# Own buffers for twiddles and sums in the Fourier pairs, the tail ahead of the next prework in the forward scan, and fold loads a block ahead

## The chip, the cores and the metric

The kernel runs on one core of a Trainium2 chip. The metric is the device time of one execution in microseconds (us). Engines are named as the profile names them: PE is the matrix engine, PEld its weight loads, DVE the vector engine, ACT the scalar (activation) engine, POOL the third one, and SP issues nearly all DMA transfers, in order, from one queue.

## The reference

One layer of an encoder, with a sequence of L = 2048 tokens and width D = 1024, in float32:

```python
h = rmsnorm(x, norm_g) * (1 + scale) + shift          # shift, scale, gate from silu(c) @ w_ada
u_f, z_f, q, k, v, r, gf_low, gb_low = split(h @ w_in)
y_f = fourier_mix(u_f, w_fmap) * silu(z_f)
y_g = gla_mix(q, k, v, gf_low, gb_low, ...) * silu(r)
x = x + gate * (concat(y_f, y_g) @ w_out)
return rmsnorm(x, final_g)
```

`fourier_mix` takes, for each of 4 groups of 256 columns, the real part of a two-dimensional Fourier transform over tokens and columns and multiplies it by a 256 x 256 map. `gla_mix` is gated linear attention with 4 heads in chunks of 64 tokens, with one scan forward and one backward over the tokens; its gates are log-sigmoids of a low-rank projection, and its output is normalized by head.

## The kernel before

**Precision and matmuls.** Matmuls run on operands split into a high and a low part (`A_hi`, `A_lo`), three passes for a product (`PASSES`). The input projection is done in bulk blocks with a seven-product scheme: `block_col` (L273, 84 matmuls of 128x512 in a block, 12 for each of the seven products) and `block_tok` (L316). Results come out of PSUM tiles `pj` through ACT and DVE. Tokens are handled in two halves, m = 1 (tokens 1024 to 2047) first, then m = 0.

**Stages.** In the order of the code: gate vectors and normalized x; `do_v(1, A, 0)`, the first half of the value projection of half 1; two calls of `fold`, which multiply the column Fourier table by the group maps (32 matmuls each, L394) and store the result in `fold_d`; `gate_sums`; `do_v(1, A, 1)`; `gate_row`; then q, k, z, r of half 1 with the first four blocks of the backward scan (`scan_back`, blocks 7 to 4) between them; then u of both halves; then the Fourier stage; the value, query and key projections of half 0; the other four blocks of the backward scan (3 to 0) with the r projection between them (`do_r`), the splitting of the output weights and first output products (`out_fourier`); and last the forward scan with the output projection.

**Order.** A list scheduler puts the instructions of all engines into an order of its own, guided by the code's order and by data and buffer dependences; so bulk matmuls of a later projection stand among those of a Fourier pair where the pair has to wait. Each engine then runs its instructions strictly in that order. All loads and stores go through SP's queue in order as well.

**The Fourier stage.** For each group g, `stage1` does additions on DVE, `do_z` projects the group's gate, and `fourier(g, Z)` runs over five pairs of residues (`PAIRS`). A step of a pair loads two operands `us` (L42), multiplies them by twiddle factors (two ACT instructions at L699 and L700, two on DVE at L701 and L702), splits the result into `gp`, multiplies by the sequence table (`pq`) and splits that into `PQ`. A pair then multiplies by the folded map `wm` into `mapA`, copies half of it (`cm`, ACT at L741), adds and subtracts (L742, L743) and multiplies both into the gate tiles Z (L744, L745). The tiles `tw` (products of a twiddle), `cm`, `wmst` (a map being staged) and `tabstg` (the table being staged) share one tag "T" with two buffers. `us0` has two buffers, `us1` one.

**The scans.** `prework` (L483 to L541) makes the decayed q and k of a block of 256 tokens for one pair of heads: a gate matmul `lg` (L491), Abs, Exp and Ln on ACT into `pa`, a running sum on DVE, and three more Exps. `pin_exp_ln` loads the table set that has both Exp and Ln; it is called in the first prework of each half's backward scan (blocks 7 and 3), and after each Silu of `sr` in blocks 8 to 15 of the forward scan. The forward scan runs over 16 blocks of 128 tokens, sc = 0 to 15: `core_fwd` (scores `sc`, outputs `on` at L766 and L768, state updates `upd`), a prework for the next 256 tokens at odd sc, `out_fwd` for the block before (48 output matmuls `po` at L836, or 96 where the Fourier half wasn't added ahead; `ahead` holds 0, 2, 5, 8, 11 and 15), and `tail_fwd`: Square on ACT with a sum, `rstd` on POOL, scaling of `o` (L804), four transposes for each pair of heads (`otr`, L808), the product with the gate tile `sr` (L810), and the split into `ghi` and `glo`. `sr` has one buffer. Table loads appear on ACT as ACT_TABLE_LOAD; the compiler puts one wherever the function needed isn't in the set that is loaded.

## Time and profile before

| | us |
|---|---|
| median of three runs | 1791.66 (1790.52 to 1793.68) |
| the profiled execution | 1784.68 |
| its span | 1782.9 |
| PE busy | 1597.6 (90%) |
| DVE busy | 1180.1 (66%) |
| ACT busy | 633.0 (36%) |
| POOL busy | 62.4 (4%) |

The profiled execution is one run with the hardware profiler on; its span runs from the first to the last record. Busy time counts the instructions that do work. "PEclk" is the share of full clock that was granted to TensorE in a stretch: a matmul takes longer where it is below 1. In the rows that list waits, the time is idle time of the waiting engine ahead of an instruction, with what ended it behind the arrow.

### The profile page before, as it was taken

To read this page: it belongs to the slowest core of one execution; us is meant where nothing else is said; L and a number is where in the kernel's file an instruction comes from. 1 tells how busy PE (TensorE), PEld (TensorE's weight loads), DVE (VectorE), ACT (ScalarE), POOL (GpSimd) and SP (SyncE) were. 2 spreads that over 40 slices of the span, in tenths; PEclk is the share of its full clock that TensorE was granted. 3 is DMA by queue.
4 is the path that set the end of the run, shared out by engine and by line. 5 is a ranking of instruction groups with operands and counts; after the bars stand their busy time and mean duration, and the time that the engine had idled before them with its cause. 6 is when DMAs were issued, how large, how long until landed. Compare 5 with 4: busy or idle time off the path is not lost. (4 is left out here: it accounts for less than half of the span.)

```text
span 1782.9 us, 25115 instructions
## 1 busy us (share of the span) xinstructions
PE 1597.6 (90%) x9012; PEld 1370.6 (77%) x9012; DVE 1180.1 (66%) x2423; ACT 633.0 (36%) x1245; POOL 62.4 (4%) x118
## 2 busy tenths in 40 slices
PE   5879899999989999999889999379998979897996
PEld 2569678778889979889878887358877868776885
DVE  4963578887579266786845454797875765677473
ACT  3632244343245011213232232663433333454342
POOL 0000000000000000000000000000010101001010
PEclk9999999999999999999999999569999989998998
DMA  7496688878975898879796867766553433434321
GB/s 286 174 402 236 245 316 307 287 281 299 349 284 203 269 337 304 270 259 328 232 300 189 283 206 234 251 206 192 182 163 108 153 96 114 146 95 133 116 89 59
DMA packets 220188, 400.42 MB, mean 225 GB/s; under 512 B 19488, under 2 KB 121632, under 8 KB 216480
## 3 DMA queue, kind: packets, MB, share of 16 engines
q1 hardware_dynamic: 219920, 398.56, 66.0%
q8 instruction: 71, 1.16, 0.3%
q14 instruction: 53, 0.43, 0.1%
q10 hardware_dynamic: 144, 0.26, 0.0%
HBM read 238.13 MB, written 160.63 MB: 224 GB/s over the span
## 5 line engine op out<-in xcount | busy, mean ns | idle before, releaser
L273 PE MATMUL pj<-A_hi,B 128*128 128x512 f32 x1344 | 438.4, 402 | 13.9 <-ACT B L48 11.3
L316 PE MATMUL pj<-B,A_hi 128*128 128x264 f32 (+1 forms) x1792 | 333.2, 287 | 17.5 <-DVE B L49 5.0
L273 PEld LDWEIGHTS pj<-A_hi,B 128*128 128x128 f32 x1344 | 253.3, 190 | 74.7 <-ACT B L48 13.1
L316 PEld LDWEIGHTS pj<-B,A_hi 128*128 128x128 f32 x1792 | 281.4, 191 | 22.1 <-DVE B L49 6.0
L273 PE MATMUL pj<-A_lo,B 128*128 128x512 f32 x672 | 268.4, 399 | 0.0
L316 PE MATMUL pj<-B,A_lo 128*128 128x264 f32 (+1 forms) x896 | 254.6, 286 | 2.3 <-DVE A_lo L49 2.3
L316 PEld LDWEIGHTS pj<-B,A_lo 128*128 128x128 f32 x896 | 171.4, 192 | 2.5 <-DVE A_lo L49 2.5
L273 PEld LDWEIGHTS pj<-A_lo,B 128*128 128x128 f32 x672 | 127.7, 190 | 27.5
L836 PE MATMUL po<-wo_hi,fhi 128*128 128x512 f32 x256 | 104.9, 411 | 9.2 <-ACT po L865 6.8
L836 PE MATMUL po<-wo_hi,ghi 128*128 128x512 f32 x256 | 105.1, 411 | 0.0
L836 PE MATMUL po<-wo_lo,ghi 128*128 128x512 f32 x256 | 103.6, 405 | 0.0
L836 PE MATMUL po<-wo_lo,fhi 128*128 128x512 f32 x256 | 102.9, 402 | 0.0
L836 PE MATMUL po<-wo_hi,flo 128*128 128x512 f32 x256 | 100.4, 403 | 0.2 <-DVE flo L49 0.2
L573 DVE SCALAR_TENSOR_TENSOR state<-state,sm,upd 128x256 f32<-128x256 f32 x112 | 48.6, 475 | 60.1 <-PE upd L56 59.8
L836 PE MATMUL po<-wo_hi,glo 128*128 128x512 f32 x256 | 84.0, 403 | 0.4 <-DVE glo L49 0.4
L277 DVE TENSOR_TENSOR u<-u,pj 128x512 f32<-128x512 f32 x96 | 65.5, 683 | 27.0 <-PE pj L273 24.6
L581 ACT ACTIVATE vh<-v 128x512 fp32r<-128x512 f32 x64 | 40.2, 628 | 106.3 <-PE upd L56 97.6
L48 ACT ACTIVATE B<-raw 128x512 fp32r<-128x512 f32 x72 | 42.8, 624 | 88.4 <-DMA raw<-in_w_in 35.0
L321 DVE TENSOR_TENSOR u<-u,pj 128x264 f32<-128x264 f32 (+1 forms) x96 | 48.6, 513 | 37.6 <-PE pj L316 37.3
L551 PE MATMUL sc<-qi,ki 128*128 128x128 f32 x256 | 58.2, 312 | 13.3 <-DVE ki L520 5.1
L56 PE MATMUL mapA<-PQ,wm 128*128 128x256 f32 x480 | 65.0, 284 | 5.0 <-DVE PQ L49 3.6
L56 PEld LDWEIGHTS mapA<-PQ,wm 128*128 128x128 f32 x480 | 61.9, 190 | 8.5 <-DVE PQ L49 4.1
(216 smaller groups left out, 3009.9 us busy)
## 6 DMA issues: line engine op xcount, KB each, us to landing
bcol_d<-B SPq DMA_DIRECT2D x84, 512.0 KB, 4.2
B<-bcol_d SPq DMA_DIRECT2D x84, 512.0 KB, 4.8
v<-v_d SPq DMA_DIRECT2D x64, 256.0 KB, 3.1
btok_d<-B SPq DMA_DIRECT2D x28, 528.0 KB, 4.0
B<-btok_d SPq DMA_DIRECT2D x28, 528.0 KB, 5.9
btok_d<-B SPq DMA_DIRECT2D x28, 512.0 KB, 4.6
B<-btok_d SPq DMA_DIRECT2D x28, 512.0 KB, 6.0
raw<-in_w_in SPq DMA_DIRECT2D x12, 1024.0 KB, 7.7
```

The lines of the kernel that those rows point to most:

```text
L48: S.activation(hi, src, AF.Copy)
L56: T.matmul(ps, a, b, start=(k == 0), stop=(k == n - 1))
L273: T.matmul(ps[:], B[k][0][:, bq, p, :], A[k][aq][:, p, :], start=(p == 0 and q == 0), stop=(p == 3 and q == 2))
L277: V.tensor_tensor(o, a, ps[:], ALU.add)
L316: T.matmul(ps[:, j, :], A[k][aq][:, p, t * P:(t + 1) * P], B[k][p // 2][:, bq, p % 2, :], start=(p == 0 and q == 0), stop=(p == 3 and q == 2))
L321: V.tensor_tensor(o[:, cut], a[:, cut], ps, ALU.add)
L551: T.matmul(ps[:, h, 0:128], ki[:, c0:c0 + P], qi[:, c0:c0 + P], start=True, stop=True)
L573: V.scalar_tensor_tensor(state[:, h, :], state[:, h, :], dec[:, g:g + 1], up_[:, h, :], ALU.mult, ALU.add)
L581: S.activation(vh[:], v[:], AF.Copy)
L836: T.matmul(ps[n][:], a, wo[j0 + j][q][:, cs], start=(first and a is yh and q == 0), stop=(last and a is yl))
```

## The change

It has four parts.

The three vectors of the first stage become slices of one tile `vecs`; the twiddle table is loaded into it later and the tile `tw` of the Fourier stage goes. The table is transposed on the way in to fit.

In the Fourier pairs `cm` gets a tag of its own with two buffers and two slots (the difference is written over the copy), so that only `tw`, `wmst` and `tabstg` share "T"; `tabstg` shrinks to 512 columns and is loaded in two pieces; `us0` goes from two buffers to one.

The fold is cut into `fold_load`, with two buffers and both loads right behind the first half of the value projection, and `fold`, which stands behind the second half.

In the forward loop `tail_fwd` follows `core_fwd` at once; its split is a function of its own, `split_y`, called after the next block's core; `out_fwd` comes last.

```diff
-    gs = cp.tile([P, KT], F32, name="gs")
-    shift = cp.tile([P, KT], F32, name="shift")
-    cact = cp.tile([P, KT], F32, name="cact")
+    vecs = cp.tile([P, 3, KT], F32, name="vecs")
+    gs, shift, cact = (vecs[:, n] for n in range(3))
...
-    def fold(gg, gw):
-        fin = gw.tile([P, 2048], F32, tag="fold", name="fold_in")
+    def fold_load(gg, gw):
+        fin = gw.tile([P, 2048], F32, tag="fold", name="fold_in", bufs=2)
...
+        return tabs, wf
+
+    def fold(gg, tabs, wf):
...
     def fourier(g, Z):
-        thi, tlo, tw = fconst["thi"], fconst["tlo"], fconst["tw"]
+        thi, tlo = fconst["thi"], fconst["tlo"]
...
-                us = [fp.tile([P, 256], F32, tag=f"us{n}", name="us", bufs=2 - n) for n, sl in enumerate(SLOT[l1]) if sl is not None]
+                us = [fp.tile([P, 256], F32, tag=f"us{n}", name="us") for n, sl in enumerate(SLOT[l1]) if sl is not None]
...
-                    c_, s_, n_ = (tw[:, l1 - 1, q:q + 1] for q in range(3))
+                    c_, s_, n_ = (vecs[:, q, l1 - 1:l1] for q in range(3))
...
-                cm = fp.tile([P, 3, 2, P], F32, tag="T", name="cm", bufs=2)
+                cm = fp.tile([P, 2, 2, P], F32, tag="cm", name="cm", bufs=2)
                 S.activation(cm[:, 0, 0:np_, :], bv, AF.Copy)
                 V.tensor_tensor(cm[:, 1, 0:np_, :], av, cm[:, 0, 0:np_, :], ALU.add)
-                V.tensor_tensor(cm[:, 2, 0:np_, :], av, cm[:, 0, 0:np_, :], ALU.subtract)
+                V.tensor_tensor(cm[:, 0, 0:np_, :], av, cm[:, 0, 0:np_, :], ALU.subtract)
                 V.tensor_tensor(z1, z1, cm[:, 1, 0:np_, :], ALU.mult)
-                V.tensor_tensor(z2, z2, cm[:, 2, 0:np_, :], ALU.mult)
+                V.tensor_tensor(z2, z2, cm[:, 0, 0:np_, :], ALU.mult)
...
     def tail_fwd(sc, os_, sr):
-        halves = []
...
             V.tensor_tensor(y, tp[:], y, ALU.mult)
+        return sr
+
+    def split_y(sr):
+        halves = []
+        for hp in range(2):
+            y = sr[:, 4 * hp:4 * hp + 4, :]
             hi = op.tile([P, 4, P], F32R, tag="ghi", name="ghi", bufs=3)
             lo = op.tile([P, 4, P], F32R, tag="glo", name="glo", bufs=2)
             split(hi[:], lo[:], y)
...
     do_v(1, A, 0)
     gw = pool(glate, "gate")
-    for g in range(2):
-        fold(g, gw)
+    folds = [fold_load(g, gw) for g in range(2)]
     acc = gate_sums(gw)
     do_v(1, A, 1)
+    for g in range(2):
+        fold(g, *folds[g])
     gate_row(acc, gw)
...
-    tw = fp.tile([P, 8, 3], F32, name="tw")
-    tabstg = fp.tile([P, 640], F32, tag="T", name="tabstg", bufs=2)
-    load(tabstg[:], i["seqtab"])
-    load(tw[:], i["tw"])
-    split(thi[:], tlo[:], tabstg[:])
-    fconst.update(thi=thi, tlo=tlo, tw=tw)
+    for cs in (slice(0, 512), slice(512, 640)):
+        tabstg = fp.tile([P, 512], F32, tag="T", name="tabstg", bufs=2)[:, 0:cs.stop - cs.start]
+        load(tabstg, i["seqtab"][:, cs])
+        split(thi[:, cs], tlo[:, cs], tabstg)
+    load(vecs[:], i["tw"])
+    fconst.update(thi=thi, tlo=tlo)
...
-    pending = None
+    sr = None
     for sc in range(16):
         if sc:
             os_ = core_fwd(sc, pre, st_f)
+            ys = split_y(sr)
+        sr = tail_fwd(sc, os_, load_sr(sc))
         if sc % 2 and sc != 15:
             gt = gates(sc // 2 + 1)
             pre = [prework(0, sc // 2 + 1, hp, gt) for hp in range(2)]
-        if pending is not None:
-            out_fwd(*pending)
-        pending = (sc, tail_fwd(sc, os_, load_sr(sc)), None if sc in ahead else load_yf(sc))
-    out_fwd(*pending)
+        if sc:
+            out_fwd(sc - 1, ys, None if sc - 1 in ahead else load_yf(sc - 1))
+    out_fwd(15, split_y(sr), None)
```

What the scheduler makes of it stands in the compiled order of each engine. PE, where the bulk projections end and the second backward scan begins, before: `pj` are bulk products, `lg`, `sc`, `ob` and `upd` belong to the scan.

```order
L273 MATMUL pj<-A_hi,B 128x512 x2
L273 MATMUL pj<-A_lo,B 128x512
L273 MATMUL pj<-A_hi,B 128x512
L491 MATMUL lg<-gt,wab_10023 128x256 x4
L551 MATMUL sc<-qi,ki 128x128
L601 MATMUL ob<-state_10036,Q 128x256 x2
L552 MATMUL sc<-Q,K 128x64
```

After, in the middle of the same scan, five of whose eight units lie in this manner among bulk products:

```order
L272 MATMUL pj<-A_hi,B 128x512 x2
L272 MATMUL pj<-A_lo,B 128x512
L272 MATMUL pj<-A_hi,B 128x512 x2
L603 MATMUL ob<-state_10038,Q 128x256 x2
L272 MATMUL pj<-A_lo,B 128x512
L272 MATMUL pj<-A_hi,B 128x512 x2
L272 MATMUL pj<-A_lo,B 128x512
L272 MATMUL pj<-A_hi,B 128x512
L493 MATMUL lg<-gt,wab_10024 128x256 x2
L56 MATMUL upd<-vh,kth 128x256
L56 MATMUL upd<-vl,kth 128x256
```

The last product of a Fourier pair (`mapA`) had 70 bulk matmuls behind it and has 460 now, and the scan's first units moved in among those.

ACT in the first preworks of that scan, before (`wo_hi` are output weights being split, `vh` values):

```order
L494 ACTIVATE pa<-lg 128x512
L481 ACT_TABLE_LOAD
L581 ACTIVATE vh<-v 128x512
L497 ACTIVATE pa<-pa 128x512
L581 ACTIVATE vh<-v 128x512
L498 ACTIVATE pa<-pa 128x512
L511 ACTIVATE sm<-sm 128x8
L475 ACTIVATE gt<-gf 128x256
L513 ACTIVATE pa<-pb 128x512
L518 ACTIVATE pb<-pb 128x512
```

After, the same preworks, with Silu of the r projection's results (L356) between them:

```order
L496 ACTIVATE pa<-lg 128x512
L483 ACT_TABLE_LOAD
L499 ACTIVATE pa<-pa 128x512
L356 ACT_TABLE_LOAD
L356 ACTIVATE st<-st 128x512
L500 ACT_TABLE_LOAD
L500 ACTIVATE pa<-pa 128x512
L477 ACTIVATE gt<-gf 128x256
L356 ACT_TABLE_LOAD
L356 ACTIVATE p_10166<-p_10166 128x512
L513 ACT_TABLE_LOAD
L513 ACTIVATE sm<-sm 128x8
```

One table load stood there and now there is one at nearly every change between Silu, Exp and Ln; in the whole program there are 68 where there were 20, 26 of the new ones in this scan and 22 in the forward scan's first half.

PE at the end of the program, where block 14's output products (`ghi`, `glo`) meet block 15's transposes (`otr`), before:

```order
L836 MATMUL po<-wo_hi_11726,glo 128x512 x2
L836 MATMUL po<-wo_hi_11726,ghi 128x512
L836 MATMUL po<-wo_lo_11727,ghi 128x512
L836 MATMUL po<-wo_hi_11726,ghi 128x512
L836 MATMUL po<-wo_lo_11727,ghi 128x512
L836 MATMUL po<-wo_hi_11726,glo 128x512 x2
L808 MATMUL otr<-ident,o 128x128 x8
L836 MATMUL po<-wo_hi_11696,ghi 128x512
L836 MATMUL po<-wo_lo_11697,ghi 128x512
L836 MATMUL po<-wo_hi_11696,ghi 128x512
```

After, the first and the second group of transposes of block 15:

```order
L768 MATMUL on<-vh,sl 128x256
L770 MATMUL on<-state_11740,Q 128x256
L843 MATMUL po<-wo_hi_11697,glo 128x512
L809 MATMUL otr<-ident,o 128x128 x4
L843 MATMUL po<-wo_hi_11697,ghi 128x512
L843 MATMUL po<-wo_lo_11698,ghi 128x512
L843 MATMUL po<-wo_hi_11697,ghi 128x512
L843 MATMUL po<-wo_lo_11698,ghi 128x512
L843 MATMUL po<-wo_hi_11697,glo 128x512 x2
```

```order
L843 MATMUL po<-wo_lo_11718,ghi 128x512
L843 MATMUL po<-wo_hi_11717,ghi 128x512
L843 MATMUL po<-wo_lo_11718,ghi 128x512
L843 MATMUL po<-wo_hi_11717,glo 128x512 x2
L809 MATMUL otr<-ident,o 128x128 x4
L843 MATMUL po<-wo_hi_11727,ghi 128x512
L843 MATMUL po<-wo_lo_11728,ghi 128x512
L843 MATMUL po<-wo_hi_11727,ghi 128x512
```

The eight transposes stood together behind all products of block 14; now 30 of those products lie between the two groups of four, and 12 behind the second.

More of the change, by code (lines that the diff above doesn't have):

```diff
@@ L899, in hybrid_kernel @@
         load(gcol[:], i["gla_g"])
-        S.activation(cact[:], ccol[:], AF.Silu)
+        S.activation(cact, ccol[:], AF.Silu)
         KO(V.tensor_scalar(b1[:], bcol[:, :, 1], 1.0, None, ALU.add))
@@ L1119, in _tables @@
     f = lambda z: np.ascontiguousarray(z, dtype=np.float32)
-    return {"seqtab": f(seq), "tw": f(tw), "chtab": f(ch), "mask": np.concatenate([mask, mask], axis=1),
+    return {"seqtab": f(seq), "tw": f(tw.transpose(0, 2, 1)), "chtab": f(ch), "mask": np.concatenate([mask, mask], axis=1),
             "sel": f(sel), "ident": np.eye(P, dtype=np.float32)}
```

## The prediction

> **What bounds the kernel now.** I read the page's engine shares and slices first, then busy time by stretch of the program, then what TensorE waits for, and last the instructions around the longest waits.
>
> ```profile
> span 1782.9 us, 25115 instructions
> PE 1597.6 (90%) x9012; PEld 1370.6 (77%) x9012; DVE 1180.1 (66%) x2423; ACT 633.0 (36%) x1245; POOL 62.4 (4%) x118
> ...
> PE   5879899999989999999889999379998979897996
> ...
> PEclk9999999999999999999999999569999989998998
> ```
>
> TensorE is busy for 90% of the span; no other engine passes 66%. 185 us are left in which PE is idle, and the slices show where: the start, one place near three fifths of the way (digits 3 and 7, with a clock of 5 and 6), and a long tail of eights. The change adds and removes no matmul, so all it can win is PE idle time and time at a low clock. By stretch (columns: length; busy time of PE, PEld, DVE, ACT, POOL; granted clock; DMA share; GB/s):
>
> ```profile
> 113.90:144.00 30.10, 17.07 (x68) 14.20 (x67) 12.25 (x16) 10.98 (x20) 0.00 (x0) 0.77 1.03 390
> 144.00:186.00 42.00, 42.00 (x341) 41.17 (x339) 16.60 (x37) 9.52 (x18) 1.64 (x1) 1.00 0.45 172
> 694.00:937.00 243.00, 225.72 (x1571) 209.10 (x1571) 175.07 (x466) 60.15 (x115) 0.00 (x0) 0.99 0.85 275
> 937.00:1111.00 174.00, 173.91 (x917) 147.78 (x915) 86.18 (x167) 47.94 (x91) 0.00 (x0) 1.00 0.72 228
> 1111.00:1196.00 85.00, 41.38 (x175) 34.08 (x175) 73.38 (x136) 53.95 (x93) 0.00 (x0) 0.65 0.73 239
> ...
> 1340.00:1745.00 405.00, 365.54 (x1838) 304.73 (x1838) 264.44 (x550) 163.00 (x370) 48.48 (x91) 0.95 0.37 116
> 1745.00:1782.90 37.90, 22.48 (x92) 17.52 (x90) 11.77 (x19) 9.48 (x21) 4.04 (x10) 0.85 0.15 53
> ```
>
> The first two rows are the map fold and the rest of the value projection; the next two the Fourier stage and the bulk projections behind it; 1111 to 1196 is the start of the second backward scan; the last two are the forward scan and its end. The costliest row by far is 1111 to 1196: 43.6 us without a matmul, and the rest at a clock of 0.65, while DVE works 73 of the 85 us. The longest single waits of PE lie in the same stretches (columns: total, times, longest):
>
> ```profile
> PE pj L394 <- DMA fold_in<-in_w_fmap: 13.0, 1, 13.0
> ...
> PE lg L491 <- DMA v<-v_d: 17.3, 1, 17.3
> PE lg L491 <- DVE pa L499: 5.0, 1, 5.0
> ...
> PE otr L808 <- DVE o L804: 12.3, 2, 6.7
> PE on L766 <- ACT sh L48: 8.2, 2, 5.2
> PE otr L808 <- DVE sr L810: 5.9, 4, 2.2
> ```
>
> **Part A, the fold.** Both loads now go out together and the 64 fold matmuls stand behind the whole value projection.
>
> ```profile
> 113.86 7.07 PE L394 MATMUL pj<-fold_in 128*128 128x256 f32 x32
> 133.96 10.08 PE L394 MATMUL pj<-fold_in 128*128 128x256 f32 x32 [13.03 <-DMA fold_in<-in_w_fmap]
> ```
>
> The second fold waits 13.03 us for a load that could only be issued when the first fold had read the single buffer, and then runs 3.01 us longer than the first, at the clock that the pause left (0.77 over the stretch). Bound of the gain: 13.03 + 3.01 = 16.0 us. Against it: DMA is saturated here (share 1.03, 390 GB/s), so the bytes of the value projection's weights, which now have to be there some 20 us earlier, were themselves on the way. I give back 5 us, a third of the bound: the stretch's DMA time is fully used, but only the part of its bytes that comes after the fold's is needed earlier. The fold's eight stores now stand in SP's queue just ahead of the gate row's; in the 42 us after 144 the DMA share is 0.45, which hides them. Moving the fold to where the projection is over costs its 14 us of matmuls there instead of here: nothing. **A = -11 us, ends -16 and 0.**
>
> **Part B, the Fourier pairs and what follows them.** Own buffers change which instruction a pair waits for. In the pairs now, ACT waits for the mapped sums ahead of the next pair's twiddles:
>
> ```profile
> ACT cm L741 <- PE mapA L56: 88.1, 32, 6.6
> ...
> ACT tw L699 <- DVE Z L745: 11.5, 13, 2.2
> SPq L42 <- ACT tw L700: 25.5, 14, 5.0
> us<-us_d SPq DMA_DIRECT2D x61, 128.0 KB, 4.2
> 694.00:1096.00 402.00, 384.72 (x2424) 345.23 (x2424) 256.15 (x623) 105.44 (x201) 0.00 (x0) 1.00 0.79 254
> 1097.00:1110.00 13.00, 13.00 (x57) 10.49 (x56) 1.00 1.02 297
> ```
>
> 88.1 us of ACT's time go into 32 waits of that kind, and the twiddle that follows waits for the last use of the shared buffer (L745). PE loses little by it, because bulk projections fill the gaps (384.7 of 402 us busy, clock 1.00); but it spreads the pairs so far that the last map product comes 70 bulk matmuls ahead of the end of the bulk. In the new order 460 stand behind it. One costs 13.0 / 57 = 0.228 us, so the pairs must end 390 x 0.228 = 89 us of PE work earlier, and those bulk matmuls then lie beside five of the eight units of the backward scan, which had none. That fills the stretch 1111 to 1196. Its 41.38 us of matmuls at clock 0.65 are 27 us at full clock; with some work at the edges that can't be hidden I count 30. Bound of the gain: 85 - 30 = 55 us; other end 0, where everything won here is lost in the pairs.
>
> What eats of it. (1) The pairs are now packed into 384.7 - 89 = 296 us of PE work. DVE's share of the old stretch is 256 us; the 89 us of bulk that leave take 89 x 16.60 / 42.00 = 35 us of DVE with them, so 221 us of DVE stand beside 296 of PE, 75%. The nearest row is 694 to 937, where DVE has 72% and PE idles 17.3 of 243 us (7%). 7% of 296 is 21 us against the 17.3 that are lost now; with the higher density I take 10 us more than now. (2) One buffer for the first operand of a twiddle: the other operand has had only one all along, so the load of each step already waits for a read; a load costs 4.2 us to landing and up to 1.8 of waiting in the queue (25.5 / 14), 36 steps x 6.0 = 216 us, inside 296. I cost it at 0, with the DVE-bound cycle as its cover; without that cover it's a rival below. (3) Three units remain behind the bulk, and the scan units among it contain new table loads, next. I take 12 us for both, about a fifth of the stretch, the nearest row being the units that had no bulk at all. The staged table is loaded in two pieces, once, ahead of the first pair, with bulk on PE: 0. The in-place subtract and the twiddles' new home change no count: 0. **B = -55 + 10 + 12 = -33 us, ends -55 and 0.**
>
> **Table loads.** Because Silus of the gate projection and the scan's Exp and Ln now alternate on ACT, the compiled order has 68 table loads where it had 20: 26 more in the backward scan, 22 in the first half of the forward scan, two in the chain of each prework there.
>
> ```profile
> 1747.04 1.28 ACT L791 ACT_TABLE_LOAD   x1 [4.78 <-DMA sr<-r_d]
> 1748.33 1.06 ACT L791 ACTIVATE sr<-sr 128x1024 f32<-128x1024 f32 x1
> 1749.41 1.28 ACT L481 ACT_TABLE_LOAD   x1
> ```
>
> 48 x 1.28 = 61 us more on ACT, which rises from 633 to about 695 us. ACT is idle for two thirds of the span, so this costs only where a chain of ACT, DVE and PE is the limit. In the forward scan a prework is covered by the 96 output matmuls of a block (22 us at 0.23), and its two extra loads are 2.6 us: mostly hidden, 6 us taken in C.
>
> The Trainium skill, page "ScalarE: Activation LUTs", section "What ACT_TABLE_LOAD costs", states about 1283 ns for the load and about 1380 ns of drain, 2.66 us for a switch; by that the 48 would be an estimated 128 us of ACT. The trace agrees with the 1283 ns, but beside these loads it has no second gap: the next instruction starts 0.01 us after a load and the next load 0.02 us after an instruction. So the sum goes by 1.28.
>
> **Part C, the forward scan.** The tail (norm, transposes, gate) now follows the block's core at once, ahead of the next prework; the hi/lo split of its result comes after the next core; the output matmuls come last.
>
> ```profile
> 1752.64 0.61 PE L836 MATMUL po<-wo_hi,glo 128*128 128x512 f32 x2
> 1759.95 1.09 PE L808 MATMUL otr<-ident,o 128*128 128x128 f32 x4 [6.69 <-DVE o L804]
> 1761.82 1.11 PE L808 MATMUL otr<-ident,o 128*128 128x128 f32 x4 [0.79 <-DVE sr L810]
> ```
>
> At the end PE finishes block 14's products, waits 6.69 us for the last normalized rows, then 0.79 us, and starts the last 48 products at a reduced clock. Now 30 products of block 14 stand between the two groups of transposes of block 15 and 12 behind the second: (30 + 12) x 0.23 = 9.7 us of cover where there was none. What is late next is the gate's tile: `sr` has one buffer, its load waits until block 14's result is split, and that split now comes after block 15's core:
>
> ```profile
> sr<-r_d SPq DMA_DIRECT2D x16, 512.0 KB, 3.6
> L791 ACT ACT_TABLE_LOAD x8 | 10.3, 1283 | 27.4 <-DMA sr<-r_d 27.4
> ```
>
> From the split on, the load takes 3.6 us, and two table loads and the Silu 1.28 + 1.06 + 1.28 = 3.6; the second group's Square stands behind them on ACT, and normalizing and transposing it takes some 3 us more (an estimate: two DVE rows and POOL). That is 10 us against the first transposes' 1.1 and 30 products' 7 us, so about 2 us of waiting remain: -5.5, and -0.5 from the clock. Of the other waits of the tail (12.3 - 6.7 = 5.6 for o, 5.1 for sr) and the 8.2 for the split scores I take half, -9; the loop's 39.5 idle us (405 - 365.54) are of many kinds, so the low end for the whole of C is -25. Against it stand +6 for the table loads. For the later split I count +1: in every block the same 10 us chain has 96 output products (22 us) as its cover, or 48 (11 us) in the six blocks whose Fourier half was added ahead. Without that cover the chain's 10 us would fall on each block; upper end +15, one us a block. **C = -6 - 9 + 7 = -8 us, ends -25 and +15.**
>
> **Sum.** -11 - 33 - 8 = -52 us. The profiled execution took 1784.7 us (span 1782.9 and 1.8 around it), so 1733 for such a one. The median of the runs shown, 1791.7, is 7.0 us above it: 1740.
>
> **Rivals.** (R1) The pairs don't get denser on the chip. For it: DVE would be at 75% beside loads that hold the SP queue; the step's budget is 296 / 36 = 8.2 us, and load and wait take 6.0 of it, so at 8.2 us a step the loads set the pace, and what is won in the scan is idle PE in the pairs. Then B is 0 and the sum is A and C: 1784.7 - 19 = 1766, 1773 as a median. Against it: the old order was slowed by a chain through ACT, not by DVE.
> (R2) Slower: the table loads lie on the path. In the backward scan PE takes its instructions in order, with bulk behind each scan matmul; if a prework that waits for tables holds up the next scan matmul, the bulk waits as well. Without tables the sum would be about -52 - 18 = -70 us (6 in C and 12 in B taken back). 48 loads spend that at 1.46 us each, 1.28 and 0.18 of hand-over; at 1.7 us the time is 1784.7 + 48 x 1.7 - 70 = 1796, 1803 as a median. For it: two loads in every prework's chain. Against it: PE has bulk or output matmuls ahead of nearly every one of them; in the first backward scan, with bulk between the units and no tables, PE is 98% busy:
>
> ```profile
> 222.00:445.00 223.00, 218.38 (x1053) 179.53 (x1052) 180.92 (x347) 92.28 (x186) 0.00 (x0) 0.99 0.84 298
> ```
>
> By the Trainium skill's 2.66 us ("ScalarE: Activation LUTs", "What ACT_TABLE_LOAD costs"), with every switch on the path, the estimate would be 128 - 70 = 58 us slower; the trace's rows above speak for the smaller price.
> (R3) The forward scan takes back what A and B give, by the chain over the single `sr` buffer: 44 / 15 = 2.9 us more for each block decide it, and then the time is the old one. For it: ACT already waits 27.4 us for these loads in 8 blocks. Against it: the cover above.
>
> **How the numbers follow.** The forecast's own case (-75 to -32 against the time before) gets 0.64; a larger gain, B and C near their bounds, 0.08; R1 and what lies near it, from -32 to -4 us, 0.18; no change, R3, 0.04; R2 0.06. A measurement of this kernel can tell about 0.2%, 3.6 us. Faster 0.90, same 0.04, slower 0.06. The range for 8 in 10 leaves out R2, R3 and the extreme gains: 1706 to 1778, which takes in R1's 1773; the forecast's own case is 1717 to 1760.
>
> **What would show it.** A: no PE gap between 110 and 140 us, fold matmuls 7 us each behind the projection. B: from the last map product to the first output product PE at least 90% busy at a clock above 0.95, the 17.3 us wait gone; the pairs at 7 to 10% PE idle. Tables: ACT near 695 us, 68 loads, and the waits for `pa` no longer than 5 us. C: the 6.69 us wait down to about 2. I am wrong if PE idles over 40 us in the Fourier stage (R1), or if PE's waits behind `pa`, `pb` or `ki` in the two scans sum to over 40 us (R2).

## The result, and the profile after

The changed kernel takes 1695.14 us (median of four runs, 1690.39 to 1696.42) against 1791.09 us for the kernel before (median of four as well): 0.9458 of its time, 95% interval 0.9437 to 0.9480. The forecast was 1740 us, in a range of 1706 to 1778: the sign was right, but the time lies below the range, and the gain, 96 us, was nearly twice the 52 us of the sum. Three later executions that took 2297 to 3165 us count in the medians given for their kernels, which they move by under 1 us, and in no ratio.

The page of the changed kernel, engine shares and slices:

```profile
span 1694.6 us, 25167 instructions
...
PE 1580.2 (93%) x9012; PEld 1358.2 (80%) x9012; DVE 1174.1 (69%) x2424; ACT 692.9 (41%) x1294; POOL 60.8 (4%) x118
...
PE   5899899999989999999999999978999999999997
...
PEclk9999999999999999999999999978999999999999
```

The hole near three fifths of the span is a shallow 7 and 8 now, and the eights of the tail are nines. PE's work is the same 9012 matmuls; its busy time fell by 17 us, and the row PEclk has fewer low digits (mean granted clock 0.954 before, 0.971 after).

For the place of the gain I cut both programs at the same three landmarks: the first product of the Fourier stage (`pq`), the last map product (`mapA`) and the first output product (`po`). Where they lie in the kernel after (the two numbers before the semicolon are first and last start):

```profile
L56 PE MATMUL pq<-thi,gp x256: 276/283/415, 679.6 to 973.3; 128*128 128x256 f32 x128
L56 PE MATMUL mapA<-PQ,wm x480: 274/283/415, 690.4 to 982.2; 128*128 128x256 f32 x160
L843 PE MATMUL po<-wo_hi,fhi x256: 388/398/795, 1129.6 to 1659.5; 128*128 128x512 f32 x128
```

The four stretches between them, before and then after (columns as above):

```profile
0.00:694.10 694.10, 628.80 (x3704) 539.43 (x3705) 458.55 (x855) 240.16 (x429) 3.48 (x6) 0.97 0.80 287
694.10:1094.30 400.20, 382.92 (x2416) 343.69 (x2415) 254.67 (x618) 105.16 (x200) 0.00 (x0) 1.00 0.79 255
1094.30:1195.90 101.60, 57.91 (x247) 47.09 (x245) 79.87 (x150) 56.88 (x97) 0.00 (x0) 0.71 0.76 245
1195.90:1782.90 587.00, 527.94 (x2650) 440.43 (x2650) 387.06 (x802) 230.78 (x519) 58.96 (x112) 0.95 0.40 127
```

```profile
0.00:679.60 679.60, 624.29 (x3704) 535.89 (x3705) 457.13 (x855) 240.74 (x429) 3.49 (x6) 0.98 0.81 293
679.60:982.20 302.60, 293.86 (x2027) 273.40 (x2026) 230.93 (x586) 93.80 (x184) 0.00 (x0) 0.98 0.80 262
982.20:1129.60 147.40, 134.23 (x635) 109.51 (x633) 86.90 (x163) 81.98 (x122) 0.00 (x0) 0.95 0.85 287
1129.60:1694.60 565.00, 527.78 (x2652) 439.41 (x2652) 399.18 (x822) 276.41 (x560) 57.36 (x112) 0.96 0.44 141
```

Up to the Fourier stage 14.5 us were won (694.1 to 679.6), from there to the first output product 51.8 (501.8 to 450.0), and from there to the end 22.0 (587.0 to 565.0). These are A, B and C of the sum, and each lies near the far end that I had given it: 16, 55 and 25. In B, PE's idle time went from 61 to 22 us and its busy time from 440.8 to 428.1 at the better clock; in C idle time went from 59.1 to 37.2 us, and its busy time stayed (527.9 and 527.8).

The waits behind these numbers. The fold, in order of time; it has no wait ahead of it now:

```profile
154.41 13.98 PE L396 MATMUL pj<-fold_in 128*128 128x256 f32 x64
```

ACT's waits in the Fourier stage, and PE's in the stretch between the last map product and the first output product:

```profile
ACT cm L743 <- PE mapA L56: 46.9, 17, 7.5
ACT tw L701 <- DMA us<-us_d: 46.4, 18, 7.7
```

```profile
PE lg L493 <- DVE pa L501: 6.3, 1, 6.3
PE ob L603 <- DVE state L575: 4.1, 1, 4.1
```

ACT waits half as long for the map products as before (88.1 us there), and more for its operands' loads (46.4 us), which is harmless: PE idles 8.7 of 302.6 us. The 17.3 us wait of `lg` is gone; 6.3 and 4.1 us are what is left at the start of the scan. In the forward part:

```profile
PE po L843 <- ACT po L872: 6.2, 5, 2.1
PE po L843 <- ACT fhi L48: 5.9, 6, 1.7
PE lg L493 <- DVE pa L501: 5.1, 2, 3.7
...
PE otr L809 <- DVE o L805: 0.6, 1, 0.6
...
PE otr L809 <- DVE sr L811: 0.5, 1, 0.5
```

Before, over the whole kernel, the last of these was

```profile
PE otr L808 <- DVE sr L810: 8.2, 6, 2.2
```

The waits ahead of `otr` fell from 20.5 us (12.3 and 8.2) to 1.1, and the one for `sh`, 8.2 us, isn't there any more.

### The profile page after: what moved, and what is told of

Read it like the earlier page. It is cut to its first block, busy times and chain, and to the rows that moved or that the text cites. A ratio compares the mean times of both kernels' runs of the same rounds, so it can differ in the third digit from the quotient of the medians.

```text
span 1694.6 us, 25167 instructions
## 1 busy us (share of the span) xinstructions
PE 1580.2 (93%) x9012; PEld 1358.2 (80%) x9012; DVE 1174.1 (69%) x2424; ACT 692.9 (41%) x1294; POOL 60.8 (4%) x118
## 5 line engine op out<-in xcount | busy, mean ns | idle before, releaser
L843 PE MATMUL po<-wo_hi,fhi 128*128 128x512 f32 x256 | 108.5, 424 | 12.1 <-ACT po L872 6.2
L843 PE MATMUL po<-wo_hi,flo 128*128 128x512 f32 x256 | 95.2, 414 | 0.2 <-DVE flo L49 0.2
L843 PE MATMUL po<-wo_hi,glo 128*128 128x512 f32 x256 | 88.6, 410 | 2.6 <-DVE glo L49 2.6
L843 PEld LDWEIGHTS po<-wo_hi,fhi 128*128 128x128 f32 x256 | 50.7, 198 | 25.8 <-ACT po L872 8.2
```

Of the source, the lines that this page charges most:

```text
L843: T.matmul(ps[n][:], a, wo[j0 + j][q][:, cs], start=(first and a is yh and q == 0), stop=(last and a is yl))
```

## The experiments

**One part at a time, and the shared buffer back.** Four kernels on one chip, beside the kernel before at 1785.95 us. The first has only this:

```diff
-        fin = gw.tile([P, 2048], F32, tag="fold", name="fold_in")
+        fin = gw.tile([P, 2048], F32, tag="fold", name="fold_in", bufs=2)
...
-    for g in range(2):
-        fold(g, gw)
+    folds = [fold_load(g, gw) for g in range(2)]
     acc = gate_sums(gw)
     do_v(1, A, 1)
+    for g in range(2):
+        fold(g, *folds[g])
```

> The kernel before with the fold's edit alone (both loads early, fold behind the second half of the value projection). Theory (the three edits are separate, and each won nearly its whole bound): the first product of the Fourier stage comes 14.5 us earlier, as in the trace after, so about 1777 us against 1791. Rival (the 16 us are handed on: the weights of the value projection arrive no earlier and the gain shown at 680 us needs the other edits): within 4 us of the time before.

Measured: 1772.58 us, ratio 0.9921 (0.9892 to 0.9950), 13.4 us less. The stretch up to the Fourier stage:

```profile
0.00:678.70 678.70, 623.56 (x3704) 536.35 (x3705) 457.79 (x855) 240.57 (x429) 3.48 (x6) 0.97 0.81 293
```

It ends at 678.7, as in the changed kernel (679.6). The theory holds, and the edit needs none of the others.

The second has the Fourier edits alone: `vecs`, `cm` with its own tag, one buffer for `us0`, the table in two pieces.

> The kernel before with the edits of the Fourier pairs alone (vecs, cm with its own buffers, one us0, table in two pieces). Theory: the stretch from the first Fourier product to the first output product is 52 us shorter, so about 1739 us; the extra table loads (69 in its order) cost nothing that shows. Rival (the extra table loads cost in the forward scan, and the forward edit hides that): the gain is under 40 us, with PE's idle time after the first output product over 65 us, against 59 before.

Measured: 1746.48 us, 0.9773 (0.9742 to 0.9805). The gain is 39.5 us, not 52. Its stretches from the Fourier stage on:

```profile
688.00:992.50 304.50, 294.42 (x2027) 273.59 (x2026) 230.77 (x586) 93.63 (x184) 0.00 (x0) 0.98 0.79 261
992.50:1139.70 147.20, 134.00 (x636) 109.33 (x634) 86.98 (x163) 81.90 (x122) 0.00 (x0) 0.96 0.85 287
1139.70:1742.60 602.90, 535.74 (x2652) 445.04 (x2652) 401.99 (x822) 278.09 (x561) 57.66 (x112) 0.94 0.40 132
```

The first two are 451.7 us together, 50 less than before, as the theory said; but the last one is 602.9 us, 16 longer than before, with 67 us of idle PE. Here the rival is right: something in the Fourier edit costs time in the forward scan.

The third has the forward loop's order alone (the last hunk of the diff, and `split_y`).

> The kernel before with the forward loop's order alone. Theory: 22 us less from the first output product to the end, about 1769 us; PE idle there falls from 59 to about 37 us. Rival (the forward gain comes from a forward scan that starts with its inputs at hand, since the backward scan moved): under 10 us.

Measured: 1748.51 us, 0.9787 (0.9751 to 0.9823): 37.4 us, more than the 22 that the traces of before and after showed for this part. PE from the first output product to the end, and its longest waits from 1195 us on:

```profile
1193.30:1745.30 552.00, 521.11 (x2650) 435.77 (x2650) 383.56 (x802) 231.61 (x519) 57.67 (x112) 0.97 0.41 135
```

```profile
PE po L841 <- ACT po L870: 4.2, 2, 2.1
PE sc L551 <- DVE sf L758: 3.9, 2, 2.1
PE otr L807 <- DVE sr L809: 2.5, 2, 1.5
```

552.0 us against 587.0. So the order is worth 35 us by itself, by this pair of profiles, and in the changed kernel (565.0) about 13 of them are missing again. The three single gains, 13.4, 39.5 and 37.4, sum to 90.3 us; the changed kernel later won 92.1 on the same measure of before (1786.49 to 1694.40): the parts add up, with the loss counted in the second.

The fourth is the changed kernel with one word different:

```diff
-                cm = fp.tile([P, 2, 2, P], F32, tag="cm", name="cm", bufs=2)
+                cm = fp.tile([P, 2, 2, P], F32, tag="T", name="cm", bufs=2)
```

> The changed kernel with cm back on the shared tag T (two slots of 512 columns, everything else as changed). Its order has 7 bulk matmuls behind the last map product (460 in the changed kernel) and 20 table loads. Theory: cm's own buffer is what lets the pairs run ahead; the 52 us of part B go, so about 1695 + 52 = 1747 us, with the hole at the start of the second backward scan back. Rival (the twiddles in vecs or the loads make the pairs denser): at most 15 us slower than the changed kernel.

Measured: 1747.60 us, 0.9783 (0.9750 to 0.9816), as expected by the theory. Its Fourier stage and the hole behind it:

```profile
677.90:1089.40 411.50, 397.65 (x2479) 357.21 (x2478) 262.48 (x625) 111.98 (x206) 0.00 (x0) 0.99 0.79 258
1089.40:1187.70 98.30, 39.83 (x185) 31.98 (x183) 72.91 (x143) 51.09 (x93) 0.00 (x0) 0.67 0.66 212
1187.70:1744.30 556.60, 520.31 (x2650) 435.00 (x2650) 384.84 (x804) 231.15 (x520) 58.00 (x112) 0.97 0.41 134
```

```profile
ACT cm L743 <- PE mapA L56: 87.3, 28, 7.1
...
ACT tw L701 <- DVE Z L747: 19.0, 12, 6.3
```

The pairs take 411.5 us in place of 302.6, the bulk is used up beside them, and the following 98.3 us have 39.8 us of matmuls at a clock of 0.67. ACT again waits 87.3 us for the map products, and the next twiddles wait 19.0 us for the last read of the sums (L747), a wait that the changed kernel doesn't have. The own tag is the cause of B, and of the extra table loads as well: this kernel has 20. Its forward part, with the new order and 20 loads, takes 556.6 us; so the order is worth 30 to 35 us, and the changed kernel lacks 8 to 13 of them.

**The table loads.** The four kernels left the question where the time in the forward scan goes, 16 us in the second of them and 8 to 13 in the changed kernel. Four kernels, beside the kernel before at 1786.38 us. A further preload in the forward scan's first prework takes 19 loads away there and hardly moves PE's order:

```diff
-        if d == 1 and hp == 0 and blk in (7, 3):
+        if hp == 0 and (d == 1 and blk in (7, 3) or d == 0 and blk == 0):
             pin_exp_ln(ab.ins)
```

> The changed kernel with one more preload of the table set that has both Exp and Ln, in the first prework of the forward scan: 49 table loads (68 in the changed kernel), all of the missing ones in the forward scan's first half; PE's order is nearly the same. Theory (the Fourier edit's 22 table loads in the forward scan cost the 13 us by which the changed kernel's forward part, 565 us, is longer than that of the forward order alone, 552 us): forward part 552 to 556 us, about 1683 us. Rival (the longer forward part comes from backward units and inputs that stand otherwise at its start; the loads are hidden, since ACT is busy for half of the time there): within 4 us of the changed kernel.

Measured: 1688.63 us, 0.9451 (0.9422 to 0.9479), between theory and rival, with a forward part of 556.5 us:

```profile
1128.90:1685.40 556.50, 521.11 (x2652) 434.68 (x2652) 399.03 (x822) 252.78 (x541) 56.07 (x112) 0.97 0.44 143
```

8.5 us shorter than the changed kernel's 565.0, though its waits by name hardly differ (5.2 for `fhi`, 6.2 for `po`): the difference is 6.7 us of PE's busy time and 1.8 of idle time. The ratio alone doesn't tell it from the changed kernel.

Next, all Silus of the gate projection moved into the forward scan:

```diff
-        do_col(m, A, blk, lambda c, b: (rd_[:, 4 * b:4 * b + 4, 2 * (blk - 12) + c, :], 4), not m)
+        do_col(m, A, blk, lambda c, b: (rd_[:, 4 * b:4 * b + 4, 2 * (blk - 12) + c, :], 4))
...
-        if sc >= 8:
-            pin_exp_ln(S.activation(sr[:], sr[:], AF.Silu).ins)
+        pin_exp_ln(S.activation(sr[:], sr[:], AF.Silu).ins)
```

> The changed kernel with all Silus of the gate projection moved to where the forward scan loads its gate tile (before, half of them stood beside the second backward scan): 36 table loads, none between the preworks' Exp and Ln, but two around a Silu in each of the 16 forward blocks. Theory (a load costs where it stands inside a prework's chain, and not beside the gate tile): the stretch from the last map product to the first output product, 147 us, gets 5 to 10 us shorter, the forward part is 555 us or less; about 1680 us. Rival (every load costs its 1.28 us of ACT somewhere in the scan): the forward part stays at 565 us, since it still has 32 loads in place of 38.

Measured: 1697.08 us, 0.9495 (0.9461 to 0.9529): no faster. Its last two stretches:

```profile
985.20:1124.10 138.90, 131.22 (x636) 108.61 (x634) 87.59 (x166) 46.63 (x86) 0.00 (x0) 0.98 0.91 303
1124.10:1692.10 568.00, 525.59 (x2652) 437.52 (x2652) 397.50 (x819) 271.47 (x557) 59.84 (x112) 0.97 0.43 141
```

The stretch before the first output product lost 8.5 us (147.4 to 138.9), with 1 load in place of 22, as the theory had it; the forward part stayed long, at 568.0 us, as the rival had it, with 32 loads in place of the 43 that stand behind the first output product in the changed kernel, and eight more Silus. So the number of loads alone doesn't set the time: this kernel has 32 fewer and isn't faster. Which of the things that moved into the forward scan took the gain back isn't separated.

Then one more preload only, behind the last Silu of the backward scan:

```diff
-        if d == 1 and hp == 0 and blk in (7, 3):
+        if (d, blk, hp) in ((1, 7, 0), (1, 3, 0), (1, 1, 1)):
```

> The changed kernel with one more preload of the table set with Exp and Ln in the prework right behind the last Silu of the backward scan: 43 table loads; those of the last three backward preworks and of the whole first half of the forward scan go. Theory: as the run with the pin in the forward scan, and 2 to 6 us more: 1678 to 1682 us. Rival (loads hidden): the changed kernel's time.

Measured: 1686.30 us, 0.9433 (0.9403 to 0.9464), above the 1678 to 1682 that I expected, with 43 loads and a forward part of 553.8 us:

```profile
1130.70:1684.50 553.80, 521.00 (x2652) 435.21 (x2652) 399.64 (x822) 245.23 (x535) 57.93 (x112) 0.97 0.44 144
```

And the kernel before with the preload of its second scan taken out, so that it has 57 loads:

```diff
-        if d == 1 and hp == 0 and blk in (7, 3):
+        if d == 1 and hp == 0 and blk == 7:
```

> The kernel before without the preload in the first prework of the second backward scan: 57 table loads where it had 20, two in each prework of the last backward units and of the forward scan's first half. Theory: the forward part gets 13 to 16 us longer and the hole ahead of the first output product some us too: 1804 to 1812 us against 1786 to 1791. Rival (hidden): within 4 us of the kernel before.

Measured: 1795.88 us, 1.0037 (1.0015 to 1.0060), slower by 9.5 us by the medians and by 6.6 by the ratio; I had expected 13 to 16 in the forward part and some more ahead of it. Its last two stretches are 107.1 and 591.4 us, against 101.6 and 587.0:

```profile
1095.80:1202.90 107.10, 59.72 (x247) 46.88 (x245) 79.92 (x150) 70.11 (x108) 0.00 (x0) 0.69 0.72 232
1202.90:1794.30 591.40, 532.78 (x2650) 444.26 (x2650) 387.83 (x802) 263.12 (x545) 57.24 (x112) 0.94 0.39 126
```

37 loads for 6.6 to 9.5 us are 0.18 to 0.26 us each on the path, of 1.28 us on ACT, and the price depends on the place. The 11 that stand ahead of the first output product cost about 5 us, half a microsecond each: that stretch took 100.3 to 102.2 us in six kernels with 20 loads and the old Fourier pairs. The other 26 can't be told from scatter: the same forward code with 20 loads took 583.2 to 589.6 us in three profiles.

**Which half of the forward order.** Two kernels from the kernel before. In one only the next prework moves behind the tail:

```diff
     for sc in range(16):
         if sc:
             os_ = core_fwd(sc, pre, st_f)
-        if sc % 2 and sc != 15:
-            gt = gates(sc // 2 + 1)
-            pre = [prework(0, sc // 2 + 1, hp, gt) for hp in range(2)]
         if pending is not None:
             out_fwd(*pending)
         pending = (sc, tail_fwd(sc, os_, load_sr(sc)), None if sc in ahead else load_yf(sc))
+        if sc % 2 and sc != 15:
+            gt = gates(sc // 2 + 1)
+            pre = [prework(0, sc // 2 + 1, hp, gt) for hp in range(2)]
```

> The kernel before, where in the forward loop only the next prework moves behind the tail: core, output products of the block before, tail with its split, prework. Theory (what PE lost in the forward scan were the waits for the transposes, 20.5 us in rows, and for the split scores, 8.2 us, because the tail stood last behind output products and prework): a part of the 35 us of the forward order comes from here, 8 to 18 us, so 1768 to 1778 us; PE's waits ahead of `otr` fall below 10 us. Rival (the split's delay alone makes the gain, by taking two instructions out of the chain from core to output products): within 4 us of the kernel before.

Measured: 1787.70 us against 1786.49, ratio 1.0003 (0.9985 to 1.0021): nothing. The waits stand where they stood:

```profile
PE otr L808 <- DVE o L804: 12.5, 2, 6.7
PE otr L808 <- DVE sr L810: 7.8, 6, 2.0
```

In the other the split alone moves behind the next core, with the tail still last:

```diff
     for sc in range(16):
         if sc:
             os_ = core_fwd(sc, pre, st_f)
+            ys = split_y(sr)
         if sc % 2 and sc != 15:
             gt = gates(sc // 2 + 1)
             pre = [prework(0, sc // 2 + 1, hp, gt) for hp in range(2)]
-        if pending is not None:
-            out_fwd(*pending)
-        pending = (sc, tail_fwd(sc, os_, load_sr(sc)), None if sc in ahead else load_yf(sc))
+        if sc:
+            out_fwd(sc - 1, ys, None if sc - 1 in ahead else load_yf(sc - 1))
+        sr = tail_fwd(sc, os_, load_sr(sc))
```

> The kernel before, where in the forward loop only the split moves behind the next block's core, and the tail stays at its old place behind the output products. Theory (the tail's place decides): within 6 us of the kernel before, with the waits ahead of `otr` still over 12 us. Rival (the split's delay alone makes it): 25 to 35 us faster.

Measured: 1792.52 us, 1.0029 (1.0015 to 1.0043), a little slower.

```profile
PE otr L807 <- DVE o L803: 9.2, 2, 6.7
...
PE otr L807 <- DVE sr L809: 7.1, 6, 1.6
```

The late split alone was expected to do little, as it does; the prework's move should have carried 8 to 18 us, and that theory fell: neither half gains anything alone. What both kernels still have is the output products of block sc - 1 written ahead of block sc's tail. That this is what counts shows in the compiled orders: a kernel that keeps the prework at its old place and only puts the tail ahead of the output products (with the late split) has, instruction for instruction on all engines, the order of the kernel with the whole forward edit, so it is the same program. The number of output products on PE ahead of a group of transposes shows what moved. For the last two blocks it was 72, 0, 48 and 0 before (the last eight transposes in one row), 72, 0, 48 and 0 with the prework moved, and 71, 23, 55 and 33 with the whole edit in the third kernel above: products now lie between the groups of transposes, where each group's normalizing takes time. That the tail ahead of the output products needs the late split I take from the buffers (`glo` has two, and both would be held by the block whose products come later); this I haven't tried.

**Changed kernel and one preload, directly.** Both on the chip of the last two:

> The changed kernel on the same chip as the next one, to compare the two directly. 1690 to 1696 us.

> The changed kernel with the one preload behind the last Silu of the backward scan, beside the changed kernel on the same chip. Theory (each of the 25 table loads that go costs 0.4 us, by the 11 us shorter forward part of its trace): 8 to 12 us faster than the changed kernel. Rival (hidden; the spans differed by chance): within 3 us.

Measured: 1694.40 us for the changed kernel, ratio 0.9480 (0.9457 to 0.9503), and 1686.55 us for the one with the preload, 0.9437 (0.9411 to 0.9463). Forward parts, first the changed kernel's:

```profile
1138.20:1700.80 562.60, 524.76 (x2652) 436.44 (x2652) 399.08 (x822) 276.48 (x560) 57.31 (x112) 0.97 0.44 142
```

```profile
1128.00:1685.80 557.80, 526.04 (x2652) 437.92 (x2652) 399.69 (x822) 245.39 (x535) 58.16 (x112) 0.96 0.45 143
```

The medians differ by 7.9 us, just under the 8 to 12 of the theory, the forward parts by 4.8. The intervals of the two ratios overlap by little, and in the other group the same kernel had 0.9433. So the sign is fairly sure and the size is not: I take the 25 loads for about 8 us, 0.3 us each, near the price in the kernel before. By its medians this is the fastest version here.

**Which half of the fold and of the Fourier edit.** Beside the kernel before at 1785.98 us. The fold with two buffers at its old place:

```diff
-        fin = gw.tile([P, 2048], F32, tag="fold", name="fold_in")
+        fin = gw.tile([P, 2048], F32, tag="fold", name="fold_in", bufs=2)
```

> The kernel before with two buffers for the fold's loads, and the fold left at its old place, ahead of the second half of the value projection. Theory (the second buffer alone takes the wait of 13 us away, since the second load then goes out with the first): the wait is gone or under 3 us and the time 10 to 14 us below the kernel before. Rival (the loads arrive too late at the old place, because the queue and the DMA engines are full there, and only the move of the matmuls behind the projection hides them): PE still waits 8 us or more ahead of the second fold, and under 6 us are won.

Measured: 1774.78 us, 0.9934 (0.9912 to 0.9955). PE's waits from 80 to 225 us, all of them:

```profile
PE pj L273 <- ACT B L48: 7.5, 1, 7.5
PE pj L316 <- DVE u L321: 1.5, 1, 1.5
PE pj L316 <- ACT st L397: 0.9, 1, 0.9
```

The 13 us wait is gone at the old place too, so the buffer is what takes it away. What the move behind the projection adds isn't settled: 2.2 us by the medians (1774.78 against 1772.58, with overlapping intervals), and 6 us by the traces, where the first product of the Fourier stage starts at 684.9 us here and at 678.7 in the kernel with the whole fold edit.

And the changed kernel with one buffer for the sums and two for the operand:

```diff
-                us = [fp.tile([P, 256], F32, tag=f"us{n}", name="us") for n, sl in enumerate(SLOT[l1]) if sl is not None]
+                us = [fp.tile([P, 256], F32, tag=f"us{n}", name="us", bufs=2 - n) for n, sl in enumerate(SLOT[l1]) if sl is not None]
...
-                cm = fp.tile([P, 2, 2, P], F32, tag="cm", name="cm", bufs=2)
+                cm = fp.tile([P, 2, 2, P], F32, tag="cm", name="cm", bufs=1)
```

> The changed kernel with one own buffer for the sums (two in the change) and two for the first twiddle operand, as before the change. Its order has 477 bulk matmuls behind the last map product, where the changed kernel has 460 and the shared tag left 7. Theory (what counts is that the sums no longer share a buffer with the twiddles, not how many they have, and the operand's buffer is hidden): within 5 us of the changed kernel, about 1690 us. Rival (the second buffer of the sums carries the gain): 20 us or more slower than the changed kernel. Rival (the single buffer of the operand costs time in the changed kernel): 5 us or more faster.

Measured: 1696.21 us, 0.9500 (0.9465 to 0.9534): the changed kernel's time within what can be told. Not sharing is what counts; a second buffer of the sums carries none of the 52 us that can be seen, and the operand's single buffer looks hidden, as the prediction had costed it. Both were changed at once, so opposite effects of a few microseconds could cancel here.

## Why the prediction was right and wrong

**Mechanisms.** All three were there: the fold's wait, the hole at the start of the second scan filled by the bulk that the pairs leave over, and the waits ahead of the transposes. The sizes were off, all in one direction.

**A, -11 taken, -14.5 measured.** The step that failed is the 5 us given back for the saturated DMA: in the changed kernel PE waits for no load between 80 and 225 us. Between 168 and 680 us it waits 5.3 us for weights (`B` from `btok_d`), where it was 0.6, but that isn't the fold's price: the kernel with the Fourier edit alone has 5.5 us of it, and the one with the fold edit alone has none, only the 4.0 us for a store of `u` that the kernel before has as well (4.1). The 14.5 us is a difference of two traces; the first product of the Fourier stage starts at 688.0 to 697.1 us in the six kernels with the old fold and at 673.7 to 682.4 in the nine profiles with the new one.

**B, -33 taken, -51.8 measured.** The bound of 55 was good. Of the two allowances, the 12 us for the units left over and the tables stood: 13.2 us of idle time remain between the last map product and the first output product (as a share, 12 us is a seventh of that stretch's 85 us and not a fifth). The one for denser pairs was wrong in sign: I added 10 us to the 17.3 that PE lost in the Fourier stage, and it lost 8.7. The density itself was worked out rightly (75%, and DVE is busy for 230.9 of 302.6 us, 76%); what was wrong was to read the 7% idle of 694 to 937 as the price of a DVE at 72%. At 76% PE idles 2.9% of the stage, and with the shared buffer back (the fourth kernel) it idles more, 13.9 us, at a DVE share of 64%. What made up the old 17.3 us is shown only in part: its longest waits were 4.7 us for a copy outside the pairs (L462) and 3.6 us for `PQ`. 27.3 forecast less 8.7 is 18.6 us, nearly all of B's miss of 18.8. R1 fell with it. Of the signs named ahead, the pairs' 7 to 10% of idle time came out at 2.9%, and one wait for `pa` is 6.3 us where none over 5 was to be.

**Table loads, 6 us taken in C and part of 12 in B.** 68 loads and an ACT at 692.9 us came as forecast (695). Loads inside a prework look like this in the changed kernel, with the counts of the lines concerned:

```profile
1270.93 0.64 ACT L499 ACTIVATE pa<-pa 128x512 f32<-128x512 f32 x1
1271.59 1.28 ACT L500 ACT_TABLE_LOAD   x1
1272.88 0.63 ACT L500 ACTIVATE pa<-pa 128x512 f32<-128x512 f32 x1
```

```profile
L500 ACT ACT_TABLE_LOAD x18 | 23.1, 1283 | 0.3
L513 ACT ACT_TABLE_LOAD x18 | 23.1, 1283 | 0.3
...
```

The next instruction starts 0.01 us after the load. The 25 loads that the preload removes all lie behind the first output product (43 there, then 18) and cost about 8 us by the medians: the 6 us were about right. With them gone the forward part (553.8 and 557.8 us in two profiles, where the changed kernel has 565.0 and 562.6) is that of the kernels with the forward order and 20 loads (552.0 and 556.6), as far as such profiles agree. R2 needed 1.46 us a load to bring the old time back, about three times the highest price that the runs show (0.5 us, ahead of the first output product). The Trainium skill ("ScalarE: Activation LUTs", "What ACT_TABLE_LOAD costs") has 2.66 us for a switch with its drain; no run here shows the second part.

**C, -8 taken, -22 measured.** This is the second big miss. Without the loads, the order is worth 30 to 35 us (the fourth and the third kernel), where I had counted 15 and taken 1 of it back for the late split. I took the whole of the last wait, but only half of the others, "of many kinds"; in fact those of `otr` and `on` (12.3, 8.2 and, from the first output product on, 8.2 us in place of the 5.9 that I had read from 1340 us on) fall from 28.7 to 2.5 us in the third kernel, and PE's busy time falls by 6.8 us at the better clock (0.95 to 0.97), which I left out but for 0.5. The chain over the single `sr` buffer, R3, is hidden: `otr` waits for `sr` 0.5 us.

**The time around the sum.** I added 7.0 us from the profiled execution to the median. The changed kernel's profiled execution took 1696.42 us, and its median was 1695.14; so the 88.3 us by which the spans differ became 96 in the medians. That part is luck: the profiled execution of the kernel before happened to be faster than the four that its median is taken from. With 3.5 in A, 18.8 in B and 14 in C this makes, to within a microsecond, the 45 us between 1740 and 1695.

**The general fault.** The bounds of A and B were right to within 4 us. That of C, 25, lies near the measured 22 by luck: it was too low for the order alone (30 to 35), and the table loads took some 8 back. Each bound was then cut, by a third to two thirds, for costs or doubts that no row showed. The range was cut once more where it left out "B and C near their bounds" with 0.08.

## What to carry to other kernels

Where unlike tiles share one rotating buffer, look for whose last read gates whose first write: giving one of them its own buffer let the scheduler run the chain ahead here and leave independent work for a later hole. Whether more buffers for the shared tag would have done the same wasn't tried. In a software pipeline, write the long-latency tail of a step ahead of the independent work that is to cover it, and see in the compiled order that this work really lies between the tail's stages. When such edits mix activation functions, count the table loads in the compiled order: one preload behind the last use of the other set gave about 8 us here.

## What the runs showed of the hardware

A Ln and the next Exp got a table load each (L500 and L513 above, 18 of each) until the set that has both was preloaded; the Trainium skill ("ScalarE: Activation LUTs", "Table sets: the hidden batching unit") says that such a pair needs one load, and here that held only where the preload stood. A load takes 1283 ns on ACT and cost 0.2 to 0.5 us of the kernel's time, by the place where it stood, so most of it was covered. And PE's busy time for the same matmuls is no constant: from the first output product to the end it was 527.9 us before and 521.1 with the forward order alone, at mean granted clocks of 0.95 and 0.97, with 28 us less idle time. That isn't a fixed rate of exchange: in the changed kernel 22 us less idle time came with the same busy time (527.8 us, clock 0.96).
